# Seven block products for the first half's down projection, SBUF accumulators for the long convolution, and a later second group of gate weights

## The chip, the cores and the metric

The program runs on one core of a Trainium2 chip, as one launch. The metric is the device time of that launch in microseconds (us). The engines are called by the profile's names: PE (TensorE; PEld is its weight load), DVE (VectorE), ACT (ScalarE), POOL (GpSimd) and SP (SyncE, which here only starts transfers).

## What is computed

A decoder trunk of one layer: 1024 rows of x behind 16 learned rows, model width 1024, hidden width of the MLP 4096, all in fp32. Cut to what the change touches:

```
u = rmsnorm(h, norm_mix_g)
x_lru, g_lru, v_cc, g_cc = split(u @ w_in)          # four times 512 columns
y_lru = rg_lru(conv4(x_lru), ...) * gelu(g_lru)     # a recurrence along the rows
c = causal_depthwise_conv(v_cc * sigmoid(g_cc), cc_conv_w, cc_conv_b)   # 31 taps
y_cc = silu(layernorm(c))
h = h + concat([rmsnorm(y_lru), rmsnorm(y_cc)]) @ w_out
h = h + square(relu(rmsnorm(h, norm_mlp_g) @ w_mlp_up)) @ w_mlp_down
out = rmsnorm(h, norm_final_g)[16:]
```

## The kernel before

**How a matmul is done.** Each fp32 operand is split into a rounded part and a remainder (`hi`, `lo`, type fp32r), and a product is three matmuls: hi by hi, hi by lo, lo by hi. So each weight tile of 512 KB takes four steps: SP starts a transfer into a `w` tile, ACT copies it into the rounded part (the cast of line 310), DVE subtracts that from the tile (the `TENSOR_TENSOR w<-w,w` of line 319, called a split below), and PE multiplies.

**The stages.** The rows are worked in two halves: A is the 16 learned rows and rows 0 to 511, B is the rest. First come the norm and the input projection, for w_in's columns in groups of 256 (`split_win`, line 544): the columns of g_cc and v_cc first, half A and half B of a group together. Then the gates and the scan of the recurrence (`lru_front`, `lru_scan`), the convolution (`conv_pair`, line 791), the layer norm of its result (`cc_finish`), and the output projection of half A (`out_proj`). Then half A's MLP, in 16 groups g of 256 hidden columns: `mlp_up` (line 1098) has 48 matmuls with 512 columns for a group, `mlp_down` (line 1124) the same number, and `mlp_down` of a group stands behind `mlp_up` of the next. DVE adds each of its eight banks to the residual `hA` (`TENSOR_TENSOR s<-mm,s`). While half A's MLP runs, DVE does half B's recurrence and convolution, and the output projection of half B is put in when g is 11 (`G_OUT`).

**Half B's MLP** is done in 8 steps q of 512 hidden columns, in 2x2 blocks with seven block products in place of eight (`up_fast`, line 1208; `down_fast`, line 1258). The four factors that are sums of weight blocks are not made by DVE: the POOL queue builds them in DRAM with transfers, eight per step and kind, of which four accumulate (`weight_sums`, line 616; `next_sum`, line 632, starts the next in the list `sums`). The factors from the activations are made and split by DVE, and DVE adds the products' banks to the residual, 14 times a step. The last down projection is not in blocks (`down_last`).

**The convolution** works on two channel tiles of 128 x 512 at a time (`conv_pair`): for each of 31 taps and each tile one DVE instruction multiplies a shifted window of the tile with the tap's weight and adds the accumulator, which is a PSUM bank with the tag `cv`. Both convolutions are background work: they have a priority behind all else.

**What sets the order.** All steps are handed to a planner (class `Plan`, line 116), which simulates the five instruction streams with a duration for each step, priorities (the place in the program, and 200000 more for background), and a number of buffers for each tag (`BUFS`: `s` are SBUF tiles of 128 x 532, `w` weight tiles, `mm`, `tr` and `cv` banks of PSUM). Each engine's stream is then written out in the order of the planned starts, and each engine works its stream in that order.

## Time and profile before

| | before |
|---|---|
| median of 3 runs | 1029.7 us (1027.03, 1029.7, 1031.1) |
| the profiled execution | 1029.11 us; its span in the profile 1027.3 us |
| granted TensorE clock, mean | 0.995 |
| PE busy | 1003.6 us, 98% of the span, 5624 matmuls |
| DVE busy | 846.6 us, 82% |
| ACT busy | 524.8 us, 51% |
| POOL busy | 150.8 us, 15% |
| the POOL queue's transfers (q0) | 76.39 MB |
| SP's transfers (q1) | 113.85 MB |

The busy time of an engine is the time in which one of its instructions was at work; PE's matmuls overlap, so that a run of equal matmuls is read by the distance of their starts. A granted clock of 1.00 is 2.4 GHz. In the views by stretch of time each row has the busy time of each engine (and in brackets its instructions), the granted clock and the share in which the core's 16 transfer engines were busy.

### The profile page before, as it was taken

The page shows a single profiled execution, that of the slowest core. Times are in us where ns is not written, and L with a number is a line of the kernel's source. Part 1 is how long each engine was busy: PE and PEld are TensorE (multiplying, and loading weights), DVE is VectorE, ACT ScalarE, POOL GpSimd, SP SyncE. Part 2 cuts the span into 40 slices and gives each one's busy share as a digit, 9 for nine tenths or more (in the row PEclk, how much of TensorE's full clock was granted, in tenths as well). Part 3 has the DMA queues.
Part 4 walks back from the last instruction along what each step waited for, and adds up shares of the span by engine and source line. Part 5 has one row for each costly group of instructions (what it writes and reads, how often), then busy time and mean ns, then how long its engine had stood idle before and what let it go on. Part 6 is the DMA issues. An engine that isn't in the chain of part 4 may idle for free.

```text
span 1027.3 us, 14822 instructions
## 1 busy us (share of the span) xinstructions
PE 1003.6 (98%) x5624; PEld 862.1 (84%) x5624; DVE 846.6 (82%) x1445; ACT 524.8 (51%) x824; POOL 150.8 (15%) x179
## 2 busy tenths in 40 slices
PE   8999999999899999999999999999999999999997
PEld 7898998977798788777888888889988989989985
DVE  6789999787889999999976565577998897897875
ACT  5822146546577633323453273347756556656544
POOL 3405443320222112222000000000000000000001
PEclk9999999999999999999999999999999999999999
DMA  9609999999999759999734232234765565565532
GB/s 288 139 8 229 275 243 275 248 291 206 220 224 251 192 156 253 242 246 271 165 105 143 80 124 83 82 121 146 248 203 187 182 193 193 171 203 184 185 103 83
DMA packets 113240, 191.19 MB, mean 186 GB/s; under 512 B 6668, under 2 KB 73244, under 8 KB 113168
## 3 DMA queue, kind: packets, MB, share of 16 engines
q0 software_dynamic: 50112, 76.39, 34.9%
q1 hardware_dynamic: 63056, 113.85, 34.0%
q8 instruction: 44, 0.72, 0.3%
q14 instruction: 28, 0.23, 0.1%
HBM read 186.02 MB, written 67.11 MB: 246 GB/s over the span
## 4 chain that ended last, share of the span: by engine, by line
PE 77%; DMA 10%; DVE 9%; ACT 2%; issue 1%; SPq 1%; ACTq 0%; DVEq 0%
PE mm L383 46%; PE mm L370 17%; PE cv L370 8%; PE tr L370 4%; DMA w<-in_w_mlp_down_dram 3%; DMA w<-in_w_out_dram 3%; DVE cv L324 3%; DMA w<-in_w_mlp_up_dram 2%; DVE s L319 2%; DVE w L319 1%; DMA s<-in_x_dram 1%; DMA w<-in_w_in_dram 1%; DVE s L324 1%; PE tr L394 1%; ACT w L310 1%
## 5 line engine op out<-in xcount | busy, mean ns | idle before, releaser
L383 PE MATMUL mm<-s,w 128*128 128x512 f32 (+2 forms) x2016 | 368.2, 342 | 1.2 <-ACT w L310 1.2
L383 PEld LDWEIGHTS mm<-s,w 128*128 128x128 f32 x2016 | 313.6, 188 | 47.0 <-ACT w L310 1.5
L383 PE MATMUL mm<-w,s 128*128 128x512 f32 (+1 forms) x1260 | 300.1, 396 | 4.6 <-DVE s L319 2.3
L310 ACT CAST w<-w 128x1024 fp32r<-128x1024 f32 x193 | 199.7, 1046 | 193.6 <-DMA w<-in_w_mlp_down_dram 61.1
L383 PEld LDWEIGHTS mm<-w,s 128*128 128x128 f32 x1260 | 235.4, 190 | 60.2 <-DVE s L319 4.4
L319 DVE TENSOR_TENSOR w<-w,w 128x1024 fp32r<-128x1024 f32 x193 | 234.7, 1218 | 44.6 <-ACT w L310 38.2
L324 DVE SCALAR_TENSOR_TENSOR cv<-c,prm,cv 128x512 f32<-128x512 f32 x232 | 174.4, 752 | 4.2
L370 PE MATMUL mm<-s,w 128*128 128x256 f32 x1152 | 140.2, 281 | 0.0
L370 PEld LDWEIGHTS mm<-s,w 128*128 128x128 f32 x1152 | 138.9, 188 | 1.3
L319 DVE TENSOR_TENSOR s<-s,s 128x512 fp32r<-128x512 f32 (+3 forms) x183 | 122.0, 684 | 20.1 <-ACT s L312 17.7
L319 DVE TENSOR_TENSOR s<-mm,s 128x512 f32<-128x512 f32 x144 | 97.0, 683 | 38.1 <-PE mm L383 17.5
L312 ACT ACTIVATE s<-s 128x512 f32<-128x512 f32 (+2 forms) x152 | 95.4, 632 | 32.9 <-DVE s L319 28.5
L370 PE MATMUL cv<-w,s 128*128 128x512 f32 x336 | 83.7, 394 | 0.0
L310 ACT CAST s<-s 128x512 fp32r<-128x512 f32 (+2 forms) x83 | 50.5, 621 | 59.7 <-DVE s L319 40.1
L319 POOL TENSOR_TENSOR s<-s,s 128x512 f32<-128x512 f32 x3 | 4.5, 1513 | 512.0 <-ACT s L312 512.0
L370 PEld LDWEIGHTS cv<-w,s 128*128 128x128 f32 x336 | 62.1, 188 | 13.6
L414 POOL DMA_DIRECT2D ws_up<-in_w_mlp_up_dram x48 | 48.7, 1166 | 44.1 <-DMA ws_up<-in_w_mlp_up_dram 25.0
L310 ACT COPY s<-mm 128x512 f32<-128x512 f32 (+2 forms) x48 | 24.4, 515 | 48.8 <-PE mm L370 33.3
L414 POOL DMA_DIRECT2D ws_down<-in_w_mlp_down_dram x42 | 38.6, 1244 | 46.3 <-DMA ws_down<-in_w_mlp_down_dram 35.8
L312 ACT ACTIVATE s<-mm 128x512 f32<-128x512 f32 x40 | 23.8, 595 | 37.2 <-PE mm L383 36.5
L370 PE MATMUL mm<-w,s 128*128 128x512 f32 x168 | 41.3, 394 | 0.0
L319 DVE TENSOR_TENSOR c<-mm,c 128x512 f32<-128x512 f32 (+2 forms) x49 | 30.9, 632 | 10.3 <-PE mm L383 10.0
(133 smaller groups left out, 723.0 us busy)
## 6 DMA issues: line engine op xcount, KB each, us to landing
w<-in_w_mlp_down_dram SPq DMA_DIRECT2D x57, 512.0 KB, 4.3
w<-in_w_mlp_up_dram SPq DMA_DIRECT2D x56, 512.0 KB, 4.7
ws_up<-in_w_mlp_up_dram POOLq DMA_DIRECT2D x48, 512.0 KB, 9.7
ws_down<-in_w_mlp_down_dram POOLq DMA_DIRECT2D x42, 512.0 KB, 10.9
w<-ws_up SPq DMA_DIRECT2D x32, 512.0 KB, 3.7
w<-ws_down SPq DMA_DIRECT2D x28, 512.0 KB, 3.7
w<-in_w_in_dram POOLq DMA_DIRECT2D x24, 512.0 KB, 10.6
ws_up<-ws_up POOLq DMA_DIRECT2D x16, 512.0 KB, 9.5
```

Of the source, the lines that this page charges most:

```text
L310: nc.scalar.copy(val(o), val(i))
L312: nc.scalar.activation(out=val(o), in_=val(i), func=func, scale=val(scale), **kw)
L319: return pl.add(eng, dur, lambda: e.tensor_tensor(out=val(o), in0=val(a), in1=val(b), op=op), refs(a, b), [o])
L324: return pl.add("dve", dur, lambda: nc.vector.scalar_tensor_tensor(out=val(o), in0=val(a), scalar=val(s), in1=val(b), op0=op0, op1=op1), r ...
L370: nc.tensor.matmul(val(p), val(a), val(b), start=start and i == 0 and k == 0, stop=k == len(pairs) - 1, skip_group_check=True)
L383: nc.tensor.matmul(val(o), val(a), val(b), start=start and k == 0, stop=stop and k == last)
L394: nc.tensor.transpose(val(o), val(i), ident.real[:rows, :rows])
L414: return pl.add("pool", 1.02, lambda: nc.gpsimd.dma_start(val(o), val(src), **kw), refs(src) + ([o] if add else []), [o], nbytes=nbytes, a ...
```

## The change

- Half A's MLP goes over 8 steps q. Step 0 is as before (`mlp_up` and `mlp_down` of groups 0 and 1). From q = 1 on, the up projection is `up_blocks`: as many matmuls as two `mlp_up` have, with the results laid out as the 2x2 blocks that `down_fast` takes; and the down projection of steps 1 to 7 is `down_fast`, with the seven products and the sums of weights of the `down` kind. The last of them stands in half B, behind `up_fast(0)`.
- The sums in DRAM are therefore wanted for both halves: the list starts with the `down` sums of steps 1 to 7, and has 16 entries instead of 15.
- `conv_pair` accumulates in SBUF tiles, which leaves the `cv` banks to `down_fast`.
- `split_win(1792)`, the second group of g_cc's columns, is planned behind the steps in `late`, which are from the first group's projection.
- 59 tiles of tag `s` instead of 54, 15 of `w` instead of 16; the gate weights of the recurrence lie in such `s` tiles.
- Half B's layer norm and output projection are put in at steps 5 and 6 (`Q_FIN`, `Q_OUT`), before at groups 8 and 11.

```diff
--- before.py
+++ after.py
@@ -51,7 +51,7 @@
 START = 0.7
 
 
-BUFS = {"s": 54, "w": 16, "c": NCT, "ty": 22, "mm": 4, "tr": 2, "cv": 2}
+BUFS = {"s": 59, "w": 15, "c": NCT, "ty": 22, "mm": 4, "tr": 2, "cv": 2}
 KEEP = {"s": 10, "w": 8, "c": 4, "ty": 6, "mm": 1, "tr": 1, "cv": 2}
 SHAPES = {"s": 532, "w": 1024, "c": 30 + T, "ty": 16, "mm": 512, "tr": 512, "cv": 512}
 PSUM_TAGS = ("mm", "tr", "cv")
@@ -60,8 +60,8 @@
 
 TABLES = {AF.Sigmoid: 1, AF.Tanh: 2, AF.Exp: 3, AF.Sqrt: 4, AF.Gelu_apprx_tanh: 5, AF.Silu: 6}
 
-G_FIN = 8
-G_OUT = 11
+Q_FIN = 5
+Q_OUT = 6
 
 
 class Buf:
@@ -627,7 +627,8 @@
         dma_pool(t[3], t[1], n, True)
         wsum[q, kind] = t
 
-    sums = [(q, kind) for q in range(NG // 2) for kind in ("up", "down")][:-1]
+    sums = [(1 + i, "down") for i in range(NG // 2 - 1)]
+    sums += [(0, "down")] + [(q, "up") for q in range(NG // 2)]
 
     def next_sum():
 
@@ -762,8 +763,7 @@
         dma_group([(rw[o * 64:(o + 1) * 64, :].view(
             lambda a, o=o: a.rearrange("p (c n) -> p c n", c=NCT)[:, :, o * 64:(o + 1) * 64]),
             src.rearrange("l (c o) i j -> (l o) i c j", o=2)[o]) for o in range(2)], 131072, late)
-        hi = cfix([P, 512], F32R, f"gw_{name}_hi")[:, 0:512]
-        lo = cfix([P, 512], F32R, f"gw_{name}_lo")[:, 0:512]
+        hi, lo = slot(F32R), slot(F32R)
         split(hi, lo, rw)
         gw[name] = (hi, lo)
 
@@ -790,7 +790,7 @@
 
     def conv_pair(cts, half, after=()):
         off = META if half == 0 else TA
-        acc = {ct: bank("cv") for ct in cts}
+        acc = {ct: slot() for ct in cts}
         for k in range(CW - 1, -1, -1):
             for ct in cts:
                 src = cbuf[ct][:, off + k:off + k + 512]
@@ -949,7 +949,7 @@
     for ct in range(2):
         v_evac(proj(wv[ct], B0), ct, B0)
     next_sum()
-    for j, w in enumerate(split_win(1792)):
+    for j, w in enumerate(split_win(1792, late)):
         for pc in PIECES:
             g_evac(proj(w, pc), 2 + j, pc)
     next_sum()
@@ -1121,6 +1121,23 @@
             hids.append(hid)
         return hids
 
+    def up_blocks(q, u2T):
+
+        h = {(t, i): slot() for t in range(2) for i in range(2)}
+        for i in range(2):
+            ws = prep_win(load_cols(w_up2, q * 512 + i * 256))
+            for j in range(2):
+                b = bank("mm")
+                pairs = []
+                for k in range(KD):
+                    hi, lo = u2T[k]
+                    whi, wlo = ws[j][k]
+                    pairs += [(whi, hi), (whi, lo), (wlo, hi)]
+                mms(b, pairs)
+                for t in range(2):
+                    act(h[t, i][:, j * 256:(j + 1) * 256], b[:, t * 256:(t + 1) * 256], AF.Relu)
+        return h
+
     def mlp_down(gs, hids, hv, done=None, last=False):
         ws = []
         for g in gs:
@@ -1380,42 +1397,42 @@
         put(1, t, 1, o1)
         put(1, t, 0, o0)
 
-    hB = u2B = None
-    todo = []
-    for g in range(NG):
-        if g % 2 == 0:
-            next_sum()
-        if g < 2:
-            if g == 0:
-                hids = mlp_up((0, 1), u2A, ((0, 256), (256, 512)))
-            hid = hids[g]
-        else:
-            hid, = mlp_up((g,), u2A, ((0, 512),))
-        todo.append((g, hid))
-        if len(todo) > 1:
-            gd, hd = todo.pop(0)
-            mlp_down((gd,), hd, hA)
-        if g == 5:
+    hids = mlp_up((0, 1), u2A, ((0, 256), (256, 512)))
+    hq = None
+    for q in range(NG // 2):
+        next_sum()
+        nxt = up_blocks(q, u2A) if q else None
+        if q == 1:
+            for g in range(2):
+                mlp_down((g,), hids[g], hA)
+        elif q > 1:
+            down_fast(q - 1, hq, hA)
+        hq = nxt
+        if q == 2:
             for h in range(2):
                 s = slot()
                 dma(s, norm_final_g[h * 512:(h + 1) * 512].partition_broadcast(P),
                     1 << 18, "pool", after=[pl.ops[-1]])
                 gf.append(s)
-        if g == G_FIN:
+        if q == Q_FIN:
             sqB = slot()
             yB = [lru_y(ct, stB[ct]["h"], sqB) for ct in range(NCT)]
             rlB = sumsq_rstd(sqB)
             ycB, rcB = cc_finish(1)
-        if g == G_OUT:
+        if q == Q_OUT:
             hBt = [pl.buf("c") for _ in range(4)]
             hB = [[t[:, 0:512], t[:, 512:1024]] for t in hBt]
             load_resid(1, hB, ())
             u2B = out_proj(1, yB, ycB, rlB, rcB, hB)
     u2 = u2_blocks(u2B)
-    hq = up_fast(0, u2)
-    gd, hd = todo.pop(0)
-    mlp_down((gd,), hd, hA, finish(0, hA))
+    nxt = up_fast(0, u2)
+    down_fast(NG // 2 - 1, hq, hA)
+    done = finish(0, hA)
+    for t in range(4):
+        done(t)
+    hq = nxt
     for q in range(1, NG // 2):
+        next_sum()
         nxt = up_fast(q, u2)
         down_fast(q - 1, hq, hB)
         hq = nxt
```

On PE, the first down projection that changes its form, that of hidden columns 512 and up: before, `mlp_down` gives each bank (`mm`) of the output six matmuls, three for each of two groups of 128 hidden rows, and has eight such banks for a group g:

```order
L383 MATMUL mm_4040<-w_3817,s_3853 128x512
L383 MATMUL mm_4040<-w_3822,s_3853 128x512
L383 MATMUL mm_4040<-w_3817,s_3860 128x512
L383 MATMUL mm_4040<-w_3857,s_3878 128x512
L383 MATMUL mm_4040<-w_3874,s_3878 128x512
L383 MATMUL mm_4040<-w_3857,s_3892 128x512
L383 MATMUL mm_4059<-w_3817,s_3853 128x512
```

In the change the same place is the start of `down_fast(1)`, whose products write `cv` banks first, then `mm`:

```order
L370 MATMUL cv_4070<-w_3823,s_3622 128x512
L370 MATMUL cv_4070<-w_3853,s_3622 128x512
L370 MATMUL cv_4070<-w_3823,s_3654 128x512
L370 MATMUL mm_4082<-w_3917,s_3741 128x512
L370 MATMUL mm_4082<-w_3921,s_3741 128x512
L370 MATMUL mm_4082<-w_3917,s_3747 128x512
L370 MATMUL mm_4082<-w_3917,s_3741 128x512
```

A bank gets six matmuls again, but 14 banks serve 512 hidden columns where 16 did before: a step has 84 matmuls in place of 96, each with 512 columns. PE's list is 84 rows shorter over all, 5652 instead of 5736.

On DVE, in the second pair of half B's convolution. Before (`c_196` is the window's source, `prm` holds the weights, `cv_4688` is the accumulator; `w` rows are splits of weights, `s<-mm,s` rows are additions to the residual):

```order
L324 SCALAR_TENSOR_TENSOR cv_4688<-c_196,prm,cv_4688 128x512 x4
L319 TENSOR_TENSOR w_4740<-w_4679,w_4725 128x1024
L324 SCALAR_TENSOR_TENSOR cv_4688<-c_196,prm,cv_4688 128x512
L319 TENSOR_TENSOR s_4757<-s_4738,s_4746 128x512
L319 TENSOR_TENSOR s_2413<-mm_4734,s_2413 128x512
L319 TENSOR_TENSOR s_2417<-mm_4753,s_2417 128x512
L324 SCALAR_TENSOR_TENSOR cv_4688<-c_196,prm,cv_4688 128x512
```

In the change the two channel tiles take turns, on the accumulators `s_4405` and `s_4407`, and the rows with `cv_4413` and `cv_4428` are additions to the residual for `down_fast(2)`:

```order
L324 SCALAR_TENSOR_TENSOR s_4407<-c_196,prm,s_4407 128x512
L324 SCALAR_TENSOR_TENSOR s_4405<-c_194,prm,s_4405 128x512
L324 SCALAR_TENSOR_TENSOR s_4407<-c_196,prm,s_4407 128x512
L324 SCALAR_TENSOR_TENSOR s_4405<-c_194,prm,s_4405 128x512
L319 TENSOR_TENSOR w_4438<-w_4403,w_4425 128x1024
L319 TENSOR_TENSOR s_2417<-cv_4413,s_2417 128x512
L319 TENSOR_TENSOR s_2426<-cv_4428,s_2426 128x512
L319 TENSOR_TENSOR s_2448<-mm_4441,s_2448 128x512
L324 SCALAR_TENSOR_TENSOR s_4407<-c_196,prm,s_4407 128x512
L319 TENSOR_TENSOR w_4473<-w_4421,w_4463 128x1024
```

Before, an accumulation often stands right behind one on the same accumulator; in the change that is rare. DVE's list has 1493 rows instead of 1332.

On DVE, at the end of half A. Before, around `mlp_down` of the last group (its first addition is the row with `mm_6733`); the weights `w_6731` and `w_6774` belong to `up_fast(1)`, and PE uses `w_6731` 96 rows behind the first matmul of `mm_6733`:

```order
L319 TENSOR_TENSOR w_6630<-w_6455,w_6499 128x1024
L319 TENSOR_TENSOR w_6658<-w_6553,w_6624 128x1024
L319 TENSOR_TENSOR w_6662<-w_6582,w_6656 128x1024
L319 TENSOR_TENSOR w_6695<-w_6626,w_6664 128x1024
L319 TENSOR_TENSOR w_6699<-w_6660,w_6697 128x1024
L319 TENSOR_TENSOR s_6620<-tr_6666,s_6620 128x512
L319 TENSOR_TENSOR w_6731<-w_6691,w_6728 128x1024
L319 TENSOR_TENSOR s_6740<-mm_6595,s_6740 128x512
L319 TENSOR_TENSOR s_2413<-mm_6733,s_2413 128x512
L319 TENSOR_TENSOR w_6774<-w_6725,w_6770 128x1024
```

In the change, around the product of `down_fast(7)` in the banks `tr_6918` and `tr_6930`; `w_6938` and `w_6962` belong to `up_fast(1)`, and PE uses `w_6938` 45 rows behind the last matmul of `tr_6918`:

```order
L319 TENSOR_TENSOR w_6916<-w_6868,w_6905 128x1024
L319 TENSOR_TENSOR s_2435<-s_2435,cv_6860 128x512
L319 TENSOR_TENSOR s_2417<-tr_6918,s_2417 128x512
L319 TENSOR_TENSOR w_6938<-w_6894,w_6926 128x1024
L319 TENSOR_TENSOR s_2426<-tr_6930,s_2426 128x512
L319 TENSOR_TENSOR s_2448<-s_2448,cv_6775 128x512
L319 TENSOR_TENSOR w_6962<-w_6914,w_6951 128x1024
L319 TENSOR_TENSOR s_2462<-s_2462,cv_6860 128x512
L319 TENSOR_TENSOR w_6977<-w_6928,w_6964 128x1024
L319 TENSOR_TENSOR s_2421<-mm_6871,s_2421 128x512
```

Before, six splits with one addition among them stand ahead of the last additions of half A; in the change splits and additions alternate.

## Rows read from the trace of the kernel before

**Rows 1.** The page, part 1 (busy time, share of the span, instructions) and part 4 (chain), by engine

```profile
PE 1003.6 (98%) x5624; PEld 862.1 (84%) x5624; DVE 846.6 (82%) x1445; ACT 524.8 (51%) x824; POOL 150.8 (15%) x179
...
PE 77%; DMA 10%; DVE 9%; ACT 2%; issue 1%; SPq 1%; ACTq 0%; DVEq 0%
```

**Rows 2.** Windows by stage: length, busy us of each engine, clock, transfer share, GB/s

```profile
0.00:60.00 60.00, 55.95 (x426) 50.02 (x427) 39.49 (x127) 41.46 (x84) 19.73 (x38) 1.00 0.73 183
...
216.00:308.00 92.00, 84.83 (x502) 72.08 (x501) 75.88 (x199) 55.92 (x109) 21.00 (x23) 0.98 1.00 230
308.00:345.00 37.00, 34.73 (x145) 27.80 (x144) 34.28 (x46) 28.94 (x43) 9.60 (x11) 0.95 0.92 221
345.00:480.00 135.00, 132.69 (x570) 106.28 (x569) 128.83 (x178) 46.90 (x61) 31.67 (x36) 1.00 0.88 226
...
690.00:1014.00 324.00, 324.00 (x2058) 292.25 (x2057) 275.23 (x402) 198.07 (x280) 2.92 (x2) 1.00 0.55 178
```

**Rows 3.** The chain of waits in order of time: start, length, what (us)

```profile
398.54 10.37 DMA w<-in_w_mlp_up_dram
...
545.17 50.20 PE mm L383 x216
...
690.72 8.50 PE mm L370 x72
```

**Rows 4.** The timeline of DVE: start, length; in brackets idle time before, and its releaser

```profile
410.03 1.22 DVE L319 TENSOR_TENSOR w<-w,w 128x1024 fp32r<-128x1024 f32 x1 [1.03 <-ACT w L310]
...
443.86 1.23 DVE L319 TENSOR_TENSOR w<-w,w 128x1024 fp32r<-128x1024 f32 x1 [1.43 <-ACT w L310]
...
467.35 1.23 DVE L319 TENSOR_TENSOR w<-w,w 128x1024 fp32r<-128x1024 f32 x1 [1.23 <-ACT w L310]
...
506.93 1.22 DVE L319 TENSOR_TENSOR w<-w,w 128x1024 fp32r<-128x1024 f32 x1
508.07 0.68 DVE L319 TENSOR_TENSOR s<-mm,s 128x512 f32<-128x512 f32 x1
508.67 0.74 DVE L324 SCALAR_TENSOR_TENSOR cv<-c,prm,cv 128x512 f32<-128x512 f32 x1
509.45 0.75 DVE L324 SCALAR_TENSOR_TENSOR c<-c,prm,cv 128x512 f32<-128x512 f32 x1
```

**Rows 5.** The timeline of PE, the same columns

```profile
411.90 1.66 PE L383 MATMUL mm<-w,s 128*128 128x512 f32 x6 [0.65 <-DVE s L319]
...
453.35 2.82 PE L383 MATMUL mm<-w,s 128*128 128x512 f32 x11 [0.93 <-DVE s L319]
...
476.72 2.62 PE L383 MATMUL mm<-w,s 128*128 128x512 f32 x10 [0.74 <-DVE s L319]
```

**Rows 6.** The timeline of DVE, two accumulating stretches, in PSUM and in SBUF

```profile
90.58 12.63 DVE L324 SCALAR_TENSOR_TENSOR cv<-c,prm,cv 128x512 f32<-128x512 f32 x16
103.12 0.42 DVE L319 TENSOR_TENSOR c<-mm,c 128x256 f32<-128x256 f32 x1
...
736.78 1.41 DVE L324 SCALAR_TENSOR_TENSOR s<-s,ty,s 128x512 f32<-128x512 f32 x2
738.11 0.68 DVE L319 TENSOR_TENSOR s<-mm,s 128x512 f32<-128x512 f32 x1
```

**Rows 7.** Transfers of 250 to 510 us by queue and issue: KB each, median us to landing

```profile
q0 software_dynamic: 20949, 35.40, 64.5%
...
w<-in_w_mlp_down_dram SPq DMA_DIRECT2D x22, 512.0 KB, 6.6
w<-in_w_mlp_up_dram SPq DMA_DIRECT2D x20, 512.0 KB, 7.6
```

**Rows 8.** The same of 520 to 1000 us

```profile
w<-in_w_mlp_down_dram SPq DMA_DIRECT2D x35, 512.0 KB, 3.7
```

**Rows 9.** Issues of line 414: duration in ns (min/median/max), first and last start in us

```profile
L414 POOL DMA_DIRECT2D ws_up<-in_w_mlp_up_dram x48: 706/1189/2333, 87.4 to 485.9; - x48
...
L414 POOL DMA_DIRECT2D ws_up<-ws_up x16: 1014/1024/1622, 107.8 to 501.9; - x16
```

## The prediction

> **What bounds the kernel now.** I read the page first. PE is busy for 1003.6 us of 1027.3, and the chain that ended last is PE's own for 77%; DVE has 82%, but not evenly [rows 1]. So the second view is the one by stage [rows 2]: look at PE's busy time against the length of the row, then at DVE's. From 690 to 1014 us, half B's MLP, PE is busy in all of the time. Before that it stands still in four places: the start (60 us with 55.95 busy), 216 to 308 (7.2 us lost), 308 to 345 (2.3, and the clock is granted at 0.95 there), and 345 to 480 (2.3). In the last of these DVE has 128.8 us of 135: half A's MLP with half B's convolution beside it is a stage in which both engines are nearly full, and it is the stage that the change rebuilds. The third view is the timeline there. A matmul with 512 columns costs PE 50.20 / 216 = 0.2324 us and one with 256 costs 8.50 / 72 = 0.118 [rows 3]. DVE has three waits for ACT's cast of a weight, of 1.03, 1.43 and 1.23 us [rows 4], and two to nine and a half microseconds behind each PE waits for DVE, for 0.65, 0.93 and 0.74 us [rows 5]. The chain says what stands behind the cast: a weight transfer of 10.37 us from 398.54 on [rows 3], then the cast, the late split at 410.03 and PE's wait that ends at 411.90 [rows 4, 5]. So a late weight passes through ACT and DVE to PE with about 0.6 of its lateness.
>
> **What the change removes on PE.** Seven steps have 84 matmuls in place of 96: 7 x 12 = 84 matmuls of 512 columns, which is the difference of PE's two lists. 84 x 0.2324 = **-19.5 us**. The up projection keeps its 96 per step. Everything that is taken away lies on the engine that sets the end, so this term counts in full unless a wait takes its place.
>
> **What it does to DVE in half A's MLP.** Start to start, DVE needs 1.14 us for a split of a weight and 0.60 for an addition or a split of 512 columns [rows 4]. A step had 8 splits of weights, 4 of activations and 16 additions, 21.1 us per 192 matmuls (44.6 us of PE). It now has 11 splits of weights, 11 differences and splits of activations and 14 additions: 11 x 1.14 + 25 x 0.60 = 27.5 us per 180 matmuls (41.8 us). That is 6.4 us more each step, beside a PE that is 2.8 us quicker.
>
> The convolution gives some of it back. An accumulation right behind one on the same accumulator costs (103.12 - 90.58) / 16 = 0.784 us in PSUM; two in SBUF on different accumulators cost (738.11 - 736.78) / 2 = 0.665 each [rows 6]. In DVE's lists 121 of the accumulations stand behind one on the same accumulator before and 10 now: 111 x 0.12 = 13 us off over both halves. No row shows a long turn of two SBUF accumulators; 0.665 to 0.784 are its bounds, and I take the lower since the row has the same operation, shape and memory.
>
> I add up both lists from the first tap of half B's convolution to its last, by the order of the change. DVE: 58 splits (66 us), 138 of 512 columns (83), 120 accumulations at 0.66 (79) and about 12 us of the recurrence: 239.8 us. PE: 984 matmuls of 512 columns and 120 of 256: 243.1 us. DVE is loaded to 98.6%. The comparable stretch before (the second pair, up to 509.45 [rows 4]) has 128.5 us of DVE in 132.7, beside 130.3 of PE: the same 98.6%, and it cost PE the 2.3 us of its three waits. So the load is not new; it lasts longer. Three waits among 23 splits cost 2.3 us, 0.10 us per split; 58 splits give 5.8, less the 2.3 that are in the time already: +3.5. The bounds: none at all is late (-2.3), or the lateness grows with SP's load. SP starts 11 loads per 41.8 us instead of 8 per 44.6, 1.47 times as many, beside the POOL queue's sums, which hold 64.5% of the transfer engines there; a load lands in 6.6 to 7.6 us there [rows 7], and in 3.7 where the POOL queue is silent [rows 8]. 1.47 x 5.8 = 8.5, less 2.3: +6.2. I take **+4**, between the proportional price and the loaded one, as the total load of the transfer engines would pass 1.0.
>
> On this point there is a rule. The Trainium skill, page "DMA: Bandwidth & Descriptors", section "Queues, rings and completion order", says that a transfer engine goes round between the queue rows that have work, a packet at a time; by it SP's row, which wants under half, would be served and the POOL queue would slow down, so the term would stay at the proportional +3.5. The trace agrees only in part: the landing times just cited nearly double beside the POOL queue.
>
> **The boundary of the halves.** Before, DVE does six splits of weights with one addition among them ahead of half A's last additions, and PE uses one of them 96 matmuls later; in the change splits and `down_fast(7)`'s additions alternate, and such a split is used 45 matmuls later (the third place in the order). Adding up, DVE is 20 to 29 us ahead of PE there before. In the change, from `down_fast(6)`'s first addition on, 70.7 us of DVE stand beside 63.4 of PE, before it gets ahead again. The price is 0 (it got ahead earlier) to 7.3 us (all of the excess); by the order DVE was no more than a few microseconds ahead, so **+3**.
>
> **Edits that I cost near nothing.** (1) The later second gate group removes three POOL transfers from the start, where SP's loads of x are under way. PE stands still for 4.05 us in the first 60 [rows 2], so no more than 4 can come back; the group's own weights could come up to 3 late: 0. (2) Half A's convolution is done some 24 us sooner in DVE's order, which can shorten the waits of 216 to 308; they come from chains through ACT and DVE in the norm and the gates rather than from the convolution. Of 7.2 us at most, I take **-1**. (3) The eight extra POOL transfers and the changed list of sums: half A's first block step comes at about 385 us. The POOL queue works its 15 sums from 87.4 to 501.9 us [rows 9], 27.6 us each, so the seven `down` entries would be there by 87.4 + 7 x 27.6 = 281. If that cover went, each missing sum would hold `down_fast` for a landing of the size in [rows 7]. (4) One `w` tile less in half B, where a load lands in 3.7 us and PE is full [rows 2, 8]: 0. (5) ACT gets 21 casts more and is at half load [rows 1]: 0. (6) The four `finish` steps in a block stand behind `down_fast(7)`, are DVE work and are in the boundary's sum.
>
> **The sum.** 1029.1 (profiled execution, 0.6 under the median of the runs) - 19.5 + 4 + 3 - 1 = **1015.6 us**. A measurement of this kernel can tell about 0.5%, some 5 us, from no change.
>
> **Rivals.**
> *DVE becomes the bound.* In the steps 1 to 5 a wait of 3.69 / 23 = 0.16 us per split [rows 4], 1.47 times as long, adds 13.6 us to DVE's 239.8: 253.4 beside 243.1, so PE loses 10.3 (less 2.3) there, and the boundary costs its full 7.3. 1029.1 - 19.5 + 8 + 7.3 - 1 = 1024. For it: DVE has no slack to catch up. Against: the DVE of the stage before had the same load, and lost 2.3.
>
> *Slower: late weights stop DVE in its order.* Each of the 58 splits stands in DVE's stream ahead of additions that PE waits for. If the contention with the POOL queue makes many of them wait, each for 1.23 us (the mean of [rows 4]), the slack of 3.3 us (243.1 - 239.8) is gone after the first three, and the rest passes to PE in full. From 20 waiting splits on nothing is won (20 x 1.23 - 3.3 = 21.3; 1029.1 - 19.5 + 21.3 - 2.3 + 3 - 1 = 1030.6); 26 of 58 give 32.0 - 3.3 = 28.7 and 1038. Only 3 of 23 wait now, so the share would have to triple.
>
> *More is won.* The POOL queue gives way, no split is late (-2.3), the boundary costs nothing and 2 us of the start come back: 1029.1 - 19.5 - 2.3 - 2 - 1 = 1004 to 1006.
>
> *The change does not do what it says*: excluded by PE's list, which has 84 matmuls less.
>
> **How the numbers follow.** Forecast 0.64 (its own range 1008 to 1023); DVE as the bound 0.18; slower 0.09; more won 0.09. The range of 1004 to 1028 takes the forecast, most of the gain case and the DVE case with 3 us of the start against it, and leaves out about 0.14. Faster by over 0.5% is below 1024.5: the forecast, the gain case and a bit over a third of the DVE case, 0.78. Slower by over 0.5% is above 1034.9: most of the third case, 0.07. The rest, 0.15, is within 0.5%.
>
> **What would show it.** PE: 84 matmuls less, and in the stretch by 25 us no idle time but short waits for DVE. DVE: over 95% busy from about 300 to 530 us, with convolution rows about 0.665 apart; if they are 0.78 apart, the second case holds. Loads of SP in 250 to 510 us landing in 7 to 9 us speak for the forecast, over 10 for the slower case, under 6 for the gain. At the boundary, near 690 us, PE should show a few waits for `TENSOR_TENSOR` of DVE where it had none. The forecast is wrong if PE's idle time outside the start grows by over 15 us or if it shrinks.

## The result: slower, and the profile of the changed kernel

The change takes 1045.2 us (1043.1 to 1047.9, 4 runs) where the kernel before takes 1029.6 (1027.0 to 1031.1, 4 runs): 1.0156 of it, with a 95% interval of 1.0125 to 1.0187. The forecast of 1015.6 us and its whole range were wrong. The profiled execution took 1047.9 us and has a span of 1046.1. The page, part 1, and by engine the chain of part 4, which reaches back to 538 us only (compare [rows 1]):

```profile
PE 995.8 (95%) x5540; PEld 854.0 (82%) x5540; DVE 874.4 (84%) x1501; ACT 553.3 (53%) x894; POOL 158.7 (15%) x187
...
PE 41%; DVE 5%; DMA 1%; issue 1%; ACT 1%; SPq 0%; ACTq 0%; DVEq 0%
```

PE works 7.8 us less than before in a span that is 18.8 longer. The windows of the change show where it stands (columns as in [rows 2]):

```profile
216.00:293.00 77.00, 63.09 (x289) 50.11 (x289) 54.03 (x151) 36.20 (x70) 21.60 (x24) 0.91 1.05 246
...
345.00:398.00 53.00, 52.07 (x223) 41.16 (x222) 53.00 (x77) 24.48 (x39) 0.00 (x0) 1.00 0.32 108
398.00:580.00 182.00, 160.01 (x673) 127.47 (x672) 155.13 (x222) 71.70 (x110) 44.43 (x48) 0.95 0.97 246
580.00:698.00 118.00, 118.00 (x544) 96.03 (x544) 92.28 (x174) 67.65 (x118) 0.00 (x0) 0.99 0.43 139
698.00:1014.00 316.00, 313.96 (x2009) 283.74 (x2009) 283.16 (x401) 198.96 (x274) 0.00 (x0) 1.00 0.59 190
```

From 345 to 398 us DVE is full and PE loses 0.9. From 398 to 580 PE stands still for 22 us and DVE, the suspected bound, for 27; the clock is granted at 0.95, and the transfer engines are full. From 580 on all is quiet again.

To add this up, both spans are cut where PE's timeline has the first matmul of half A's MLP (284.28 and 293.09 us) and that of half B's (690.56 and 698.30):

| us | before | change | matmuls alone | lost |
|---|---|---|---|---|
| up to half A's MLP | 284.3 | 293.1 | 0 | +8.8 |
| half A's MLP | 406.3 | 405.2 | -120 x 0.2324 = -27.9 | +26.8 |
| half B's MLP to the end | 336.7 | 347.8 | +36 x 0.2324 = +8.4 | +2.7 |

(The last down projection of half A now stands in half B's part: 84 matmuls there instead of 48.) The removed 19.5 us are there; 38.3 came back, 26.8 of them in half A's MLP.

**One loss, followed back.** The timeline of the change by engine; the columns are those of [rows 4]:

```profile
428.90 0.38 SPq L400 DMA_DIRECT2D w<-in_w_mlp_down_dram  x1
...
430.37 4.72 DVE L324 SCALAR_TENSOR_TENSOR s<-c,prm,s 128x512 f32<-128x512 f32 x7
...
437.87 1.04 ACT L310 CAST w<-w 128x1024 fp32r<-128x1024 f32 x1 [8.38 <-DMA w<-in_w_mlp_down_dram]
...
438.94 1.22 DVE L319 TENSOR_TENSOR w<-w,w 128x1024 fp32r<-128x1024 f32 x1 [3.85 <-ACT w L310]
440.09 1.28 DVE L319 TENSOR_TENSOR s<-cv,s 128x512 f32<-128x512 f32 x2
...
440.83 5.44 PE L370 MATMUL cv<-w,s 128*128 128x512 f32 x12 [6.47 <-DVE s L319]
446.10 2.94 PE L370 MATMUL tr<-w,s 128*128 128x512 f32 x12
...
537.27 5.03 PE L370 MATMUL cv<-w,s 128*128 128x512 f32 x12 [7.30 <-DVE s L319]
...
576.63 0.48 PE L394 MATMUL tr<-ident,c 128*128 128x128 f32 x1 [5.89 <-DVE c L324]
```

ACT stands for 8.38 us until a load that SP starts at 428.90 is there, and casts it at 437.87. DVE has stood for 3.85 us in front of its split, behind which stand the two additions that free PE's `cv` bank, and PE has stood for 6.47. Then PE pays again: the next 12 matmuls take 5.44 us where the 12 behind them take 2.94. The granted clock is 0.50 from 440.8 to 446.1 us, the lower of its two levels (1.2 and 2.4 GHz), and 1.00 again from 446.1 on. The same happens at 537.27; at 576.63 PE waits for the last tap of the convolution itself, which the late splits have pushed back. The waits of 300 to 600 us, before and then in the change (us in total, times, longest):

```profile
DVE w L319 <- ACT w L310: 9.9, 11, 2.2
```

```profile
DVE w L319 <- ACT w L310: 24.9, 13, 6.2
```

Not many more splits wait; each waits twice as long (1.9 us in the mean, before 0.9).

**Why the loads are late.** Transfers by queue, before from 345 to 500 us and in the change from 398 to 575 (packets, MB, share of 16 engines), and there the loads of the up weights:

```profile
q0 software_dynamic: 12182, 21.10, 62.5%
q1 hardware_dynamic: 9374, 14.65, 27.5%
```

```profile
q0 software_dynamic: 15778, 24.43, 65.4%
q1 hardware_dynamic: 11567, 19.99, 33.6%
...
w<-in_w_mlp_up_dram SPq DMA_DIRECT2D x12, 512.0 KB, 11.5
```

Both queues fill 99% of the engines in the change, 90% before. But the window of before holds the two stands of POOL's stream that are shown below, in which its queue runs dry. Where the sums run without such a stand, before from 394 to 502 us and then in the change from 414 to 570, the engines are full in both kernels:

```profile
q0 software_dynamic: 9728, 16.78, 72.1%
q1 hardware_dynamic: 6593, 9.99, 27.2%
...
w<-in_w_mlp_up_dram SPq DMA_DIRECT2D x10, 512.0 KB, 7.0
```

```profile
q0 software_dynamic: 14554, 22.19, 67.9%
q1 hardware_dynamic: 10540, 17.36, 33.2%
...
w<-in_w_mlp_up_dram SPq DMA_DIRECT2D x12, 512.0 KB, 11.5
```

There the POOL queue moves 155 GB/s before and 142 in the change, SP's queue 93 and 111. So engines that are full beside the sums are not new. What is new is that SP asks for more at the same time, and that its up loads land in 11.5 us instead of 7.0. Over the whole 177 us of the change SP moves 19.99 MB, 113 GB/s; without the sums it takes 135, as an experiment below shows.

**Why the sums are there.** The POOL timeline of the change, and of the kernel before:

```profile
398.46 0.56 POOL L400 DMA_DIRECT2D s<-in_norm_final_g_dram  x1 [81.68 <-PE tr L370]
399.01 2.72 POOL L414 DMA_DIRECT2D ws_up<-in_w_mlp_up_dram  x3
...
569.73 1.02 POOL L414 DMA_DIRECT2D ws_up<-ws_up  x1 [4.94 <-DMA ws_up<-ws_up]
```

```profile
367.75 0.56 POOL L400 DMA_DIRECT2D s<-in_norm_final_g_dram  x1 [24.30 <-PE mm L383]
...
384.05 0.57 POOL L400 DMA_DIRECT2D s<-in_norm_final_g_dram  x1 [13.04 <-DVE s L319]
```

The load of the final norm's gains into a busy `s` tile stands in POOL's stream for 81.7 us with the up sums behind it. So 316 to 398 us, which could have taken three of them, is quiet (transfer share 0.32 from 345 on), and the sums run back to back through the block steps, until 569.73.

### The profile page after: what moved, and what is told of

Same layout as the page of the kernel before. It is cut to its first block, busy times and chain, and to the rows that moved or that the text cites. A ratio compares the mean times of both kernels' runs of the same rounds, so it can differ in the third digit from the quotient of the medians.

```text
span 1046.1 us, 14868 instructions
## 1 busy us (share of the span) xinstructions
PE 995.8 (95%) x5540; PEld 854.0 (82%) x5540; DVE 874.4 (84%) x1501; ACT 553.3 (53%) x894; POOL 158.7 (15%) x187
## 5 line engine op out<-in xcount | busy, mean ns | idle before, releaser
L319 DVE TENSOR_TENSOR w<-w,w 128x1024 fp32r<-128x1024 f32 x214 | 259.5, 1218 | 69.4 <-ACT w L310 64.3
L370 PE MATMUL cv<-w,s 128*128 128x512 f32 x672 | 171.9, 403 | 16.3 <-DVE s L319 16.2
L324 DVE SCALAR_TENSOR_TENSOR s<-c,prm,s 128x512 f32<-128x512 f32 (+1 forms) x240 | 167.6, 743 | 0.4
L370 PEld LDWEIGHTS cv<-w,s 128*128 128x128 f32 x672 | 127.6, 193 | 47.5 <-DVE s L319 17.5
L319 DVE TENSOR_TENSOR s<-s,s 128x512 fp32r<-128x512 f32 (+4 forms) x234 | 155.1, 684 | 11.6 <-ACT s L312 8.6
L383 PE MATMUL mm<-w,s 128*128 128x512 f32 (+1 forms) x588 | 140.7, 397 | 0.8 <-DVE s L319 0.5
L383 PEld LDWEIGHTS mm<-w,s 128*128 128x128 f32 x588 | 109.9, 192 | 26.9 <-DVE s L319 1.4
L310 ACT CAST s<-s 128x512 fp32r<-128x512 f32 (+2 forms) x134 | 79.8, 620 | 43.8 <-DVE s L319 28.6
L370 PE MATMUL mm<-w,s 128*128 128x512 f32 x336 | 82.9, 395 | 0.0
L370 PEld LDWEIGHTS mm<-w,s 128*128 128x128 f32 x336 | 62.9, 188 | 14.8
L319 DVE TENSOR_TENSOR s<-mm,s 128x512 f32<-128x512 f32 x60 | 40.8, 683 | 14.7 <-PE mm L370 8.6
```

The source lines that it names most:

```text
L310: nc.scalar.copy(val(o), val(i))
L319: return pl.add(eng, dur, lambda: e.tensor_tensor(out=val(o), in0=val(a), in1=val(b), op=op), refs(a, b), [o])
L324: return pl.add("dve", dur, lambda: nc.vector.scalar_tensor_tensor(out=val(o), in0=val(a), scalar=val(s), in1=val(b), op0=op0, op1=op1), r ...
L370: nc.tensor.matmul(val(p), val(a), val(b), start=start and i == 0 and k == 0, stop=k == len(pairs) - 1, skip_group_check=True)
L383: nc.tensor.matmul(val(o), val(a), val(b), start=start and k == 0, stop=stop and k == last)
```

## Experiments

The theory: the up sums' transfers beside the block steps delay SP's weights, and DVE, which has no slack and works in order, hands the delay to PE. Rivals: too few `w` tiles; DVE's load by itself; the sums' mere amount. Each kernel has one profiled execution. In the three runs below that change the kernel before in half A's MLP alone, the stage ahead of it still ends between 279.2 and 285.1 us (284.3 before), so a few microseconds in one stage tell nothing. "Half A's MLP" is the second stage of the table above, in the profiled execution (before 406.3, the change 405.2, without any loss 373). Ratios are to the kernel before on the same chip, with 95% intervals.

**What the loss needs.** One more weight tile:

```diff
-BUFS = {"s": 59, "w": 15, "c": NCT, "ty": 22, "mm": 4, "tr": 2, "cv": 2}
+BUFS = {"s": 59, "w": 16, "c": NCT, "ty": 10, "mm": 4, "tr": 2, "cv": 2}
```

> The change with one weight tile more (16 w tiles, paid for with 10 instead of 22 of the tiny ty tiles). Tile-chain theory: with 15 tiles many loads go into the tile that the split just before has freed, so a load waits for the landing, cast and split of an earlier one; one tile more takes away most of these chains outside half A's MLP and a third of them in it, so about 9 us of the waits of 216 to 317 us and 5 to 10 us of those of 400 to 580 come back: 1025 to 1034. Crowded-transfer theory (the sums of the POOL queue alone make the loads late): tiles do not matter, 1042 to 1048. DVE theory (DVE has too much work in half A's MLP): 1042 to 1048.

1046.1 us, 1.021 [1.0154, 1.0267]: nothing comes back in the median, and the splits wait 23.9 us in 10 waits. The profiled execution, the fastest of four that lie between 1040.8 and 1055.3, has 395.8 us for half A's MLP, so some microseconds for one tile are not excluded; but as the median does not move, the missing tile does not explain the loss.

The gains loaded behind half A's loop, so that nothing blocks POOL's stream:

```diff
-        if q == 2:
-            for h in range(2):
-                s = slot()
-                dma(s, norm_final_g[...
...
+    for h in range(2):
+        t = slot()
+        dma(t, norm_final_g[...
```

> The change with the two loads of the final norm's gains moved from step 2 of half A's MLP to the end of half A, so that the POOL queue does not stand behind them from 317 to 398 us. Crowded-transfer theory: the sums of the up kind run from 317 us on and end some 80 us earlier, so the contention covers only half of the block steps; about half of the 26 us lost in half A's MLP comes back: 1030 to 1036. Tile-chain theory: the chains stay, and only the later ones find empty transfer engines; 1034 to 1043. DVE theory: 1043 to 1047.

1034.3 us, 1.0072 [1.0043, 1.010]. Half A's MLP 390.3, splits wait 12.7 us. With the sums free to start at once, half A's MLP gets 15 us back and the whole some 9 (1.0156 less 1.0072); half B's part loses some (352.0), as the last sum now stands behind the gains (POOL starts it at 677 us).

The up sums left out:

```diff
-    sums += [(0, "down")] + [(q, "up") for q in range(NG // 2)]
+    sums += [(0, "down")]
...
-        src = wsum[q, kind][n]
+        src = wsum[q, "down"][n]
```

> The change without the sums of the up kind: half B's up projection reads the down sums in their place, so 64 POOL transfers are left out and half B's products have other factors. Crowded-transfer theory: the loads of half A's MLP land in about 4 us, nearly all of the 26 us come back: 1018 to 1024. Tile-chain theory: the chain needs late landings to hurt, so here too most comes back, 1020 to 1030, but SP's waits for DVE's splits stay as many; were the chains enough by themselves, over 1035. DVE theory: 1042 to 1047, PE waits for DVE in the same places.

Half B's products read the `down` sums in their place, so SP's loads stay as many. 1005.0 us, 0.9798 [0.9778, 0.9818]. Half A's MLP 373.4. Its window of 320 to 510 us:

```profile
320.00:510.00 190.00, 189.54 (x814) 152.37 (x813) 190.00 (x265) 94.95 (x150) 1.16 (x2) 1.00 0.40 132
```

DVE is busy in every microsecond and PE loses 0.5. So a full DVE by itself costs nothing, and the loss needs the sums. Its transfers of 385 to 560 us give SP's want:

```profile
q1 hardware_dynamic: 13483, 23.57, 41.0%
...
w<-in_w_mlp_up_dram SPq DMA_DIRECT2D x12, 512.0 KB, 3.7
```

23.57 MB in 175 us is 135 GB/s. With the sums' 65.4% that makes 106% of the engines. At 113 instead of 135 GB/s the 177 us of the change hold 177 x (1 - 113/135) = 29 us too much, about the 26.8 lost. This shows no cause, though: a step loads the same weights however long it lasts, so any loss of this length would bring SP's rate down to the same figure.

DVE given slack, with the sums as they are: half of half B's taps left out, some 40 us of DVE.

```diff
-        for k in range(CW - 1, -1, -1):
+        for k in (range(CW - 1, -1, -1) if half == 0 else range(CW - 1, -1, -2)):
```

> The change with 16 of the 31 taps in half B's convolution (the other 15 are left out of the result), 60 accumulations of 0.66 us or 40 us of DVE's work less in half A's MLP. DVE theory: most of the 26 us lost there comes back, 1018 to 1028. Tile-chain and crowded-transfer theories: DVE was waiting for weights, not short of time; a few us come back, 1038 to 1046.

1033.5 us, 1.0068 [1.0039, 1.0097]; half A's MLP 390.7. The splits wait longer than ever (44.9 us, 18 times) and PE loses half as much (17 us over the 373, instead of 32): slack of DVE takes lateness up, and in the change it has next to none.

**Does more load, or fewer tiles, do the same to the kernel before?** 21 further 512 KB transfers on SP's queue, whose data nobody uses; four `w` tiles held back through half A's MLP; and both:

```diff
+        if g >= 2 and g % 2 == 0:
+            for n in range(3):
+                t = pl.fixed(dr.tile([P, 1024], F32, name=f"extra_{g}_{n}"))[:, 0:1024]
+                dma(t.view(k4), w_up2[...], 1 << 19, "sp", [...])
```

> The kernel before with 21 more transfers of 512 KB, three for every two groups of half A's MLP, from DRAM to DRAM on SP's queue, their result unused: the transfers that the block steps add, without their casts, splits, tiles and additions. Crowded-transfer theory: PE's waits between 345 and 510 us grow, 1034 to 1050. Theory that traffic alone is harmless, and the change needs DVE's fuller stream or the tile chains to lose time: 1026 to 1032.

```diff
+    pins = [wtile(F32) for _ in range(4)]
```

> The kernel before with four of its 16 weight tiles held idle through half A's MLP, so that in the planned order a weight's load starts 22 us ahead of PE's first use of it (median) instead of 34; the change has 21. Same matmuls, same DVE work, same transfers as before. Lead theory (a load that starts so late cannot take the landing times beside the sums): 1040 to 1055, with PE waits of several us for DVE between 380 and 510 us. Theory that the block steps' own DVE work or transfers are what loses the time: 1026 to 1033.

> The kernel before with both edits of e8 and e9: four weight tiles held idle in half A's MLP, and 21 more transfers of 512 KB on SP's queue. Alone the one cost nothing and the other some 4 us. If it is the two together (more loads on a shorter lead) that make the change's weights late: 1040 or more, DVE's waits for ACT's cast in 300 to 600 us at 20 us or more (9.9 before, 24.9 in the change). If they only add: 1032 to 1037.

0.9998 [0.9963, 1.0033]; 1.0032 [0.9998, 1.0066]; 1.0054 [1.0026, 1.0081]. The collapse that the theories put at 1034, 1040 and 1040 us or more is not seen in any of them. Half A's MLP takes 405.8, 415.0 and 414.3 us (406.3 before): the extra transfers cost nothing there, and the shorter lead of the loads some 8 us, of which the whole run shows 3 to 6. In the first, SP's queue moved 18.84 MB in 155 us (122 GB/s) at 93% of the engines. The extra transfers took 15.6 us each, the kernel's own loads 9.5 and 7.1 (before 6.4 and 6.6): most of the lateness fell on transfers that nobody waits for. From 394 to 502 us its queues hold:

```profile
q0 software_dynamic: 8697, 15.76, 65.0%
q1 hardware_dynamic: 9672, 12.86, 34.6%
```

These are the shares of the change. The engines are as full, SP's queue moves 119 GB/s, and PE loses 1.8 us in these 108 (before 2.3). So engines that are full with sums and loads are not enough by themselves, and 113 GB/s is no limit for SP's queue beside the sums. Whether this kernel is spared because its own weights were not the late ones, or because they are loaded further ahead, the run does not tell.

**Moving the sums.** Up sums behind gates, which are an ACT copy of one column that POOL reads: 3 sums from half A's MLP on, 2 behind half B's layer norm, 3 in half B; the gains late. The same without the later fetch of the gate weights, and with 2 + 2 + 4:

```diff
+    def gated_sums(n, src):
+        g, o = cfix([P, 1], F32, f"gate_{len(ups)}"), cfix([P, 1], F32, f"gated_{len(ups)}")
+        act(g[:, 0:1], src, AF.Copy)
+        with prio(BG):
+            op = tt(o[:, 0:1], g[:, 0:1], g[:, 0:1], ALU.add, "pool")
+            for _ in range(n):
+                weight_sums(*ups.pop(0), [op])
```

> The change with the up sums gated: three of them start when half A's MLP begins (a tiny ACT copy that POOL reads), two when half B's layer norm is done, one at each of the first three steps of half B; the final gains are loaded at the end of half A. All sums are made. Crowded-transfer theory: from 390 to 580 us no sum runs beside the block steps and none from 240 to 290 us, so the time comes near the 1005 us of the kernel without up sums: 1004 to 1014. Tile-chain theory: 1020 to 1030, as the chains are still there. DVE theory (too much DVE work in half A's MLP): 1025 to 1035.

```diff
-    for j, w in enumerate(split_win(1792, late)):
+    for j, w in enumerate(split_win(1792)):
```

> The gated kernel with the second group of gate weights fetched early again, as before the change. If the later fetch is neutral: within 3 us of the gated kernel; if it pushed the POOL queue's work into the waits of 216 to 290 us, 3 to 8 us faster; if it did what it is for, 3 to 8 us slower.

> The gated kernel with two sums at the start of half A's MLP, two behind half B's layer norm and four in half B. Crowded-transfer theory: equal to the gated kernel or up to 4 us faster if its third sum still runs beside the first block step; a sum in half B costs nothing as the transfer engines are half free there: within 4 us of the gated kernel. If sums in half B cost what they cost in half A: 5 us slower.

1043.7 us, 1.0127 [1.0077, 1.0178]; 1050.0, 1.0186 [1.0142, 1.023]; 1043.9, 1.0126 [1.0077, 1.0174]: far above the 1004 to 1014 expected of the first. A gate alone moves the loss: half A's MLP falls to 397.3, but half B's part grows from 347.8 to 365.4, where three of the sums now run. A gate also releases many copies at once (ten in one issue row from 297.56 us on in the first), and PE still has waits of 5.75 us for ACT and 4.96 for DVE in half A's MLP. The second run's median is some 6 us above the first's, but the intervals overlap, and the stage ahead of the MLP, in which the fetch lies, ends at 284.6 against 284.9 us: what the later fetch is worth is not shown.

Each sum's transfers one by one instead of four copies at once, with the gains late:

```diff
-        for o, src in ((t[0], x), (t[1], z), (t[2], x), (t[3], v)):
-            dma_pool(o.view(k), blk(q, *src), n, after=after)
...
+        for o, src, add in ((t[0], x, y), (t[2], x, z), (t[1], z, t[0]), (t[3], v, t[1])):
+            after = [dma_pool(o.view(k), blk(q, *src), n, after=after)]
...
+            after = [dma_pool(o.view(k), blk(q, *add), n, True, after)]
```

> The change with the final gains loaded at the end of half A and the eight transfers of each sum in pairs of a copy and the accumulation that waits for it, so that about two of them are under way at a time instead of four. If the depth of the POOL queue's bursts makes the loads late: loads land in 4 to 6 us and the time is 1012 to 1026. If only the total traffic counts: within 4 us of the kernel with the gains moved alone (1034).

1029.2 us, 0.9981 [0.9941, 1.0021]; half A's MLP 387.2. So 18 us of half A's MLP are back, 15 of them by the later gains; by the ratios (1.0072 less 0.9981) the pairs are worth some 9 us with the same bytes moved, and the kernel is level with the one before. This lies between its two forecasts (1012 to 1026 if the bursts count, 1030 to 1038 if only the traffic does).

Steps 1 and 2 as before the change, blocks from step 3 on, the sums for them in order of use; without and with the pairs of the run above:

```diff
-    sums = [(1 + i, "down") for i in range(NG // 2 - 1)]
+    sums = [(q, "down") for q in range(3, NG // 2)]
+    for q in range(NG // 2):
+        sums += [(q, "up")] + ([(q, "down")] if q < 3 else [])
```

> The change with blocks from step 3 on alone (steps 1 and 2 as before; five down projections in blocks, 60 matmuls or 13.9 us less than before in place of 19.5) and the final gains loaded at the end of half A. Lead theory: the long lead is kept until the sums have ended near 460 to 500 us, so little is lost in the steps: 1014 to 1024. If the loss comes with any block step: 1028 to 1036.

> The kernel with blocks from step 3 on and with the sums' transfers in pairs. Lead theory: as without the pairs or a few us better, 1010 to 1022.

1.0049 [1.0021, 1.0076] and 1.0028 [0.9994, 1.0063]: no better than the runs that they vary, within their intervals. The 1014 to 1024 and 1010 to 1022 that a longer lead was to give are missed.

The gains in tiles of their own, which never block; the same in pairs; the same with half B's convolution dealt over all seven steps:

```diff
-    gf = []
+    gf = [cfix([P, 512], F32, f"gf_{h}")[:, 0:512] for h in range(2)]
```

> The change with the final gains in two tiles of their own (and 10 instead of 22 tiny tiles), so that no POOL transfer waits for a tile: the sums go on from 317 us and none is behind the gains at the end of half A. Crowded-transfer theory: as e2 in half A's MLP and without its 6 us at the boundary of the halves: 1024 to 1032.

> The same with the sums' transfers in pairs (e10's edit). e10 was at 1029 with about 6 us lost behind the late gains; 1019 to 1027.

> The same with half B's convolution dealt out in the plan over seven steps (18 accumulations a step; layer norm and output projection of half B one step later), so that DVE is planned at about 94% instead of 98.6% of PE's time in the block steps. In-order theory (a late weight stops a DVE that has no slack): most of what is left of the loss there goes, 1008 to 1018. If DVE's slack does not matter: as e15, or slower where the boundary of the halves gets fuller.

1.0098 [1.0064, 1.0133]; 1.0006 [0.9972, 1.0041]; 0.9982 [0.9945, 1.0019]. By the ratios pairs give some 9 us again (1.0098 less 1.0006), with intervals that do not meet. The first two are above their forecasts. Spreading DVE's load gives nothing that can be told in the whole: half A's MLP is 381.3 instead of 393.5 in the profiled executions, but the stage ahead of it is 9 us longer.

All of it together: gains in tiles of their own, pairs, each sum behind the one before, four up sums from the start of half A's MLP on, and the rest behind half B's layer norm:

```diff
+    ups.insert(4, (0, "down"))
...
+    gated_sums(4, u2A[KD - 1][0].f32[:, 511:512])
...
+            gated_sums(len(ups), ycB[0][0].f32[:, 0:1])
```

> All sums made, in the stretches where SP wants little: the first seven down sums as before; four up sums from the end of half A's output projection on (about 290 to 400 us), one behind the other and with their transfers in pairs; the last down sum and four up sums only when half B's layer norm is done (about 590 us on); the final gains in tiles of their own. Rate theory (SP and the POOL queue together want more than the transfer engines move, from 400 to 575 us): that stretch is free of sums, so 1010 to 1022. If sums cost the same wherever they run beside block steps and in half B: 1028 to 1040.

1023.3 us (1022.1 to 1025.0), **0.991 [0.988, 0.994]**: the one version with all the sums that beats both kernels, though 1 us above the forecast. Its windows and two POOL rows:

```profile
290.00:398.00 108.00, 107.51 (x564) 90.75 (x563) 104.06 (x169) 69.86 (x120) 19.86 (x22) 1.00 0.75 195
398.00:580.00 182.00, 179.23 (x794) 145.01 (x792) 174.61 (x267) 88.16 (x135) 11.59 (x13) 0.99 0.58 172
...
668.00:1010.00 342.00, 335.49 (x2086) 302.08 (x2087) 291.58 (x421) 206.61 (x288) 24.71 (x25) 0.99 0.70 213
```

```profile
302.18 0.19 POOL L319 TENSOR_TENSOR gated<-gate 128x1 f32<-128x1 f32 x1 [39.27 <-ACT gate L310]
...
582.64 0.68 POOL L319 TENSOR_TENSOR gated<-gate 128x1 f32<-128x1 f32 x1 [132.61 <-ACT gate L310]
```

From 302 to 448 us four sums run one transfer or two at a time (the transfer share is 0.75 from 290 to 398); then the queue waits, the share from 398 to 580 is 0.58 instead of 0.97, and PE loses 2.8 us there instead of 22. Half A's MLP takes 377.7. What it does not get: half B's part takes 355.8 with the sums that were moved there, and the stage ahead of the MLP 289.7.

Last, is it the rate or the bunches? The up sums without their accumulating transfers, half the POOL queue's traffic:

```diff
+        if kind == "up":
+            wsum[q, kind] = t
+            return
```

> The change with the four copies of each up sum alone: the four accumulating transfers are left out, so half B's products have other factors. The copies are still started four at a time, at the same places of the order. Rate theory: the POOL queue wants about half as much, SP gets the 135 GB/s that it moves without up sums, DVE's waits for the cast in 300 to 600 us fall from 24.9 to under 10 us: 1006 to 1022. If the four copies at a time are what makes the loads late: 1030 or more.

1036.0 us, 1.0037 [1.0007, 1.0068], half A's MLP 393.7: the forecast by the rate, 1006 to 1022, is missed. Over 398 to 575 us the POOL queue holds 20.3% of the engines and SP's 35.4%, 56% together, and half A's MLP still lies 20 us over the 373. So a sum of shares over the stage does not decide. The waits between the accumulations had spaced the copies; without them nine went out in one issue row at 412 us. From 420 to 448 the engines were full (77.9% and 23.2%), three up loads took 22.6 us (median) to land, and PE has one long wait (PE's timeline) and hardly another until 462:

```profile
447.04 5.49 PE L370 MATMUL cv<-w,s 128*128 128x512 f32 x12 [12.39 <-DVE s L319]
...
462.81 1.64 PE L370 MATMUL cv<-w,s 128*128 128x512 f32 x6 [0.50 <-DVE s L319]
```

## Why the prediction was wrong

*The removed matmuls, -19.5: right.* PE's list is 84 shorter, and without the up sums the kernel is 21 us under the one before (1026.0 to 1005.0); a few of these may be losses that the kernel before had from the sums itself.

*The convolution in SBUF: right.* Seven accumulations in 4.72 us are 0.67 each; the prediction took 0.665. So "DVE becomes the bound" is out, and the run without sums shows DVE full at no cost.

*The boundary, +3: right in size, by luck.* The half B part lost 2.7 us. But where the prediction looked for it, PE has a single wait for DVE, of 0.72 us at 699; the other wait of this part, 1.31 us at 755, is for a cast of ACT.

***The failed step: "I take +4"* for DVE's stretch and the late weights.** Half A's MLP lost 26.8. The prediction priced lateness by the number of splits, 0.10 us each, and raised it by SP's 1.47 times as many loads. What the runs show in its place: the up sums beside the block steps make weights late, and the lateness is not paid by the split. A late weight stops DVE in its order, and PE behind it, in few long stops: PE's are of 6.47, 7.30 and 5.89 us, and behind the first two its granted clock is 0.50 and 0.54 for some 5 us. Without the up sums PE loses 0.5 us in 190 there; with most of them moved out of 398 to 580 us, 2.8 in 182.

The reason given for +4, that "the total load of the transfer engines would pass 1.0", does not set the two kernels apart: before, from 394 to 502 us, the engines were already 99% full, and PE lost 2.3. Why the same kind of sums costs the block steps so much more is shown in part only. With DVE's work cut the loss in half A's MLP is halved, but with the work only spread the whole gains nothing; a shorter lead costs the kernel before some 8 us in half A's MLP; and sums issued in pairs cost 9 us less with the same bytes. The budget of 65% and 41%, 106%, fits the loss, but the run with extra transfers (full engines, nothing lost) and the run with copies alone (56% in the mean, 20 us lost) do not bear it out as a rule. How much belongs to each stays open.

*Edit (3), costed at nothing: the second half of the same mistake.* The `down` sums are in time, as was said (the last issue of the seven is at 245.99 us). Where the up sums then run was not asked. The trace of before had the two rows that show POOL's stream standing behind the gains, 24.30 and 13.04 us; the change made that 81.7 and pushed the sums onto the stretch where SP wants most. The run with the gains moved gives some 9 us back.

*Edits (1) and (2), 0 and -1: measured +8.8 ahead of the MLP.* The three waits of PE in 216 to 293 us for ACT and DVE are longer (13.9 us lost, 7.2 before), and the granted clock there is 0.91. The later fetch is not what costs it, as far as the run without it shows, in which the stage ends at 284.6 us (284.9 with it). In the run without up sums and the three with gates, which have none in that stretch, the stage ends at 281 to 285 us. But in the best version, without them too, it ends at 289.7, and in the run with pairs and gains in tiles of their own, which has them there, at 284.6. This stays open.

*The rule weighed.* By the Trainium skill, page "DMA: Bandwidth & Descriptors", section "Queues, rings and completion order", a transfer engine goes round between the queue rows that have work, a packet at a time. The trace agrees in part: the POOL queue did slow, from 155 to 142 GB/s, and to 146 beside the extra transfers; but SP's up loads landed in 11.5 us instead of 7.0, so to be served is not to be in time. What decides the shares was not tested.

*The slower rival* had the mechanism: late weights stop DVE in its order. It asked for 20 waiting splits of 1.23 us; it was 13 with a mean of 1.9. Its 0.09 rested on "the share would have to triple", a count of waits, and a count does not show how long each can get. Its 1031 to 1038 lie under the 1045, and the 8.8 us ahead of the MLP are not in them. The main sign post worked: PE's idle time outside the first 60 us grew by 27 us, over the 15. Two others did not: DVE was 89% busy from 300 to 530 us, not over 95, as it stood waiting, and the up loads took 9.2 us from 250 to 510, under the "over 10" of the slower case, since that window holds the quiet stretch.

## What to carry to other kernels

Before work is made denser, look in each stage at what else is moving, in windows without idle stretches in them: a mean over a window with a pause hides that the engines are full. Where they are, a price per load that was read from another stage need not hold; ask how far ahead of its use each load starts, and whether the engine that waits for it can catch up. Give background transfers to stretches with room, a few at a time, and look at what stands behind a load that waits for a busy tile on the same queue. An engine that is 100% busy may be harmless, as DVE was without the up sums; an engine with no slack that works in order turns the late operand of one step into a stop for all that follow.

## What was not expected of the hardware

- The queue of sums from DRAM to DRAM gives way only a little when SP asks for more on full engines: 155 GB/s before, 142 in the change and 146 with extra transfers on SP's queue, while the landing of SP's up loads goes from 3.7 us (without the sums) to 7.0 before and 11.5 in the change.
- A stop of PE is paid 1.3 to 1.4 times: behind the waits of 6.47 and 7.30 us, 12 matmuls took 5.44 and 5.03 us where 2.94 is usual. Behind a shorter wait the addition can be as large: in the run with the gains moved, 12 matmuls behind a wait of 2.82 us took 5.49.
- Kernels with sums beside half A's MLP scatter: 10 runs of the one with pairs and late gains lie between 1021.8 and 1037.0 us, 13 of the kernel before on one chip between 1022.6 and 1035.6, the 4 without up sums between 1003.6 and 1005.6.
